# Layer two of a streaming-encoder trunk: two products of the values' pair between the gate block's halves, and the two 264-column blocks as one pair of seven products

## The chip, the cores and the metric

One core of one Trainium2 chip runs the whole program. The metric is device time in microseconds (us). TensorE (PE) multiplies; a matmul has a stationary operand loaded into the array ("LDWEIGHTS", PEld in the profile) and a moving one. VectorE (DVE) and ScalarE (ACT) do elementwise work, GpSimd (POOL) a few small operations and the stores of token sums, SyncE (SP) issues the loads.

## The reference

Two layers (DEPTH = 2) on x of 512 tokens by 2048 features. In each layer one input projection makes all of z = h @ w_in; the columns are queries, keys, values and gates of two head groups.

```python
def hybrid_layer(x, w_in, w_out, g_pre, g_post, w_alpha, b_alpha, g_gla, g_att, rel_bias):
    h = rmsnorm(x, g_pre)
    z = h @ w_in
    gq, gk, gv, gg, ga, aq, ak, av, ag = split_columns(z)
    log_a = jax.nn.log_sigmoid((ga @ w_alpha + b_alpha)) / GLA_TAU
    o_gla = gla_chunk_causal(gq, gk, gv, log_a)        # recurrence over chunks of 64 tokens
    o_gla = rmsnorm(o_gla, g_gla) * jax.nn.silu(gg)
    o_att = chunk_band_attention(aq, ak, av, rel_bias)  # softmax over 9 chunks
    o_att = rmsnorm(o_att, g_att) * jax.nn.silu(ag)
    y = jnp.concatenate([o_gla, o_att], axis=-1) @ w_out
    return x + rmsnorm(y, g_post)
```

## The kernel before

**Numbers.** Every product is made from high and low parts: a weight chunk w is cast to `wh` by ScalarE, VectorE makes `wl` = w − `wh`, and token operands are split in the same way (`split`, a ScalarE cast and a VectorE subtraction on line 109). A product then takes three matmuls: wh·a_hi, wl·a_hi, wh·a_lo. A weight chunk is 256 features (two runs of 128) by 512 columns, kept as a tile of 128 x 1024.

**Column blocks.** The input projection's columns are cut into blocks: AG0 (512 columns of the attention group's gates), AG1 and AG2 (264 columns each: the rest of the gates, and the 16 columns of the low-rank forget gate in AG2), and six pairs of 512-column blocks, `PAIRS`, the first of which, (AV0, AV1), is the attention values, the second and third the queries and keys.

**Two kinds of product.** `std_gemm` multiplies one block plainly: 8 chunks of features in the order `CO`, with 6 matmuls for each chunk and tile of 128 tokens (line 328). `fast_gemm` multiplies a pair of blocks by a scheme of seven products in place of eight: the tokens are cut into half 0 and half 1 (256 each), the features into a top and a bottom half, and the pair gives two column halves. P1 and P2 take the operands of half 0 and half 1 as they are, or weights added up; P5, P6, P3, P7 take sums and differences of token operands called S1, S2, S4, S3; P4 takes A22 itself. Each product runs over 4 chunks c0 to c3, so a pair is 28 jobs of 12 matmuls (line 406, or 396 when the roles of tokens and weights are exchanged). Accumulators X and Y (two PSUM tiles each) take turns, and finished products are copied out by ScalarE or combined by VectorE.

**Token operands.** Half 0's and half 1's operands are tiles named a11c, a12c (half 0) and g or sa tiles (half 1), made by `prep_half` from PE transposes. `make_sums` makes S1 to S4 for each chunk: a VectorE subtraction or addition (lines 588, 591, 594, 597), a split, and a store to DRAM on POOL's queue (S<-g). Some sums also keep a `home` in SBUF; the others go through slots named in `STAGE`, and each product that needs a sum reads it back on SP (sa<-S, ring of 4).

**Order of the work.** All weight chunks are jobs in one list, `stream`. `take` hands out the next job, and `ahead` keeps the coming jobs' loads (SP, into the ring raw of 5 or the ring H of 4), high parts (ring wh of 4) and low parts (ring wl of 3) three to five jobs ahead. Other work (sums, gates, attention) are generators in `tasks`, moved on by `pump` at a `rate` per step of a product. A scheduler below this language then fixes each engine's order. `tc.issue_after` forces one instruction behind another.

Layer two (l = 1) before: AG0 and AG1 over the two token tiles of half 0, the same over half 1 with the token sums as a task, AG2 over all four tiles with the last two chunks tile by tile (`lag=2`), then the task `forget_gate`, the load of ScalarE's table for exponentials (`act_table`), the values' pair, the query and key pairs, and the rest. In layer one the three blocks run over all four tiles, with the token sums beside AG1.

Of the kernel before, what the change touches and what calls it, by code (L numbers as in the profile page):

```python
# [16 lines left out]
L = 2  # L17
# [19 lines left out]
def hybrid_trunk(  # L37
# [109 lines left out]
    class Job:  # L147
        def __init__(self, l, kind, c, b0, b1=None, pair=None):
            self.l, self.kind, self.c, self.b0, self.b1, self.pair = l, kind, c, b0, b1, pair
            self.a = None  # L150

        def cut(self, tile_):
# [17 lines left out]
        def load(self):  # L170
            k, c, p, b0, b1 = self.kind, self.c, self.pair, self.b0, self.b1
            end = b0 >= NB_IN and k != "std"
            if end:
                c = OC[c]
            top, bottom = (c + 4, c) if end else (c, c + 4)
            mid = end and b0 == W23[0] and self.l < L - 1
            if k == "std":
                self.raw = self.fetch(rtile("raw", bufs=5), b0, c)
            elif k == "P1":
                p["H", self.c] = self.fetch(rtile("H"), b0, top)  # L180
                last_h[0] = last_load[0]
            elif k == "P5":
                p["r", self.c] = self.fetch(rtile("raw", bufs=5), b1, top)
            elif k == "P6":
                p["r", self.c] = self.fetch(rtile("raw", bufs=5), b1, bottom)
            elif k == "P7":
                p["r", self.c] = p.pop(("t", self.c), None) or self.fetch(rtile("raw", bufs=5), b0, top)
            elif k == "P2" or (k == "P4" and end):
# [3 lines left out]
            if src is not None and b0 != NB_IN and not (k == "P5" and b0 == AV0):  # L192
                until(lambda: k == "P4" or (id(sums), LEFT[k], c) in written)
                self.a = rtile("sa", (2, 512), F32R)
                with tc.issue_after(last_h[0]) if mid else nullcontext():
                    last_load[0] = nc.sync.dma_start(flat(self.a), src).ins
            if b0 == W23[0] and k == ("P6" if mid else "P5"):
                with tc.issue_after(last_h[0]):
                    p["t", self.c] = self.fetch(slot(f"a11{self.c}" if mid else SPARE[self.c], [2, 512]), b0, c + 4)

        def high(self):
            k, c, p = self.kind, self.c, self.pair
            if k == "std":
                src = self.raw
            else:
                h, r = p["H", c], p.get(("r", c))
                src = h if k in ("P1", "P5", "P6", "P4") else r
                early = k in ("P7", "P4") and self.b0 == W23[0] and self.l < L - 1
                with tc.issue_after(lows[-4 if early else -2]) if self.b0 >= NB_IN else nullcontext():
                    if k in ("P5", "P6") or (k == "P4" and self.b0 >= NB_IN):  # L210
                        nc.vector.tensor_tensor(out=h, in0=h, in1=r, op=ALU.add)  # L211
                    elif k == "P7":
                        nc.vector.tensor_tensor(out=r, in0=h, in1=r, op=ALU.subtract)  # L213
# [8 lines left out]
        def low(self):  # L222
# [7 lines left out]
            lows.append(last_low[0])  # L230
            if self.kind == "P2" and self.b0 < NB_IN:
                h = self.pair["H", self.c]
                nc.vector.tensor_tensor(out=h, in0=h, in1=self.src, op=ALU.add)  # L233

    stream = []
    for l in range(L):
        if l:
            stream += [Job(l, "std", c, b) for b in (AG0, AG1, AG0, AG1, AG2) for c in CO]
        else:
            stream += [Job(l, "std", c, b) for b in (AG0, AG1, AG2) for c in CO]  # L240
        for b0, b1 in PAIRS:
            pr = {}
            stream += [Job(l, k, c, b0, b1, pr) for k, c in PROD]
# [97 lines left out]

    def fast_gemm(l, pair, consume, rate=0.0, skip=0, feature_major=False, after=None, end=False, lag=0, ops=A):
        b0 = pair[0]
        acc = {n: [ps_mm.tile([P, W], F32, tag="mm", name=nm("mm")) for _ in range(2)] for n in roles[0]}
        roles.reverse()
        target = {"P1": "X", "P5": "Y", "P6": "X", "P3": "Y", "P7": "X", "P2": "Y", "P4": "X"}
        starts = ["P1", "P5", "P2"]
        if end:
            target.update(P2="Z")
        prod = (PROD_OUT if b0 == NB_IN else PROD_END) if end else PROD  # L350
        pace = Pace(rate, skip)
        keep = {}

        def copies(name, src):
            keep[name] = []
            for t in range(2):
                e = ev()
                last_copy[0] = nc.scalar.copy(e, src[t]).ins  # L358
# [8 lines left out]
        def finished(k, t):  # L367
            x_, y_ = acc["X"][t], acc["Y"][t]
            if k == "P3":
                consume(1, 0, t, None, combine(y_, keep["x"][t], ALU.subtract, keep["x"][t]))  # L370
            elif k == "P7":
                src = keep["x"][t] if end else x_
                consume(1, 1, t, None, combine(keep["p5"][t], src, ALU.subtract, keep["p5"][t]))
# [38 lines left out]
        for k, c in prod:  # L412
            if k == "P2" and end and c == 0:
                acc["Z"] = [aux(), aux()]
            if lag and k == "P4" and c == 4 - lag:
# [12 lines left out]
            if c == 3:  # L428
                if k == "P1":
                    copies("p1", acc["X"])  # L430
                elif k == "P5":
                    copies("p5", acc["Y"])
                elif k == "P6":
                    copies("x", acc["X"])
                else:
                    if k == "P7" and end:
                        copies("x", acc["X"])
                    for t in range(2):
# [31 lines left out]
    STAGE = ("g6", "g7", "g4", "g5", "g10")  # L470
    HOME = {("S1", c): tag for c, tag in enumerate(("g9", "g14", "g15", "g2"))}
    XS0 = (("g16", "g17"), ("g12", "g13"))
    XS1 = ("g9", "g10")
# [91 lines left out]

    def make_sums(dst, tags, parts, home={}, chunks=range(4)):
        stage = [0]

        def put(name, c, src):
# [10 lines left out]

        for c in chunks:
            got = parts(c)
            while got is None:
                yield
                got = parts(c)
            a11, a12, a21, a22 = got
            yield
            nc.vector.tensor_tensor(out=a22, in0=a21, in1=a22, op=ALU.subtract)
            put("S1", c, a22)
            yield  # L590
            nc.vector.tensor_tensor(out=a21, in0=a11, in1=a21, op=ALU.subtract)
            put("S3", c, a21)
# [8 lines left out]
    def token_sums(l):  # L601
        return make_sums(sa_d[l], STAGE, lambda c: (full[0, c][:, 0, :], full[0, c][:, 1, :], full[1, c][:, 0, :], full[1, c][:, 1, :]), HOME)

# [44 lines left out]
    def first_scales():  # L648
# [13 lines left out]
        nc.scalar.copy(rb, ps)  # L662

    def first_operands():
        ends = []
        for ch in CO:
# [71 lines left out]
    def layer(l):  # L738
# [111 lines left out]

        if l:
            for half in range(2):
                for q, b in enumerate((AG0, AG1)):
                    std_gemm(
                        l, b, (2 * half, 2 * half + 1), CO, operand_in, gate_evac(q), rate=0.7 if q else 1.3,
                    )
                if half == 0:
                    tasks.append(token_sums(l))
            std_gemm(l, AG2, range(NT), CO, operand_in, gate_evac(2), rate=0.7, lag=2)
        else:  # L860
# [4 lines left out]
        drain()  # L865
        tasks.append(forget_gate())
        act_table("natural_log_exp_and_others")

# [3 lines left out]
        def av_consume(j, h, t, src, comb):  # L872
            if (j, h) not in av:
                av[j, h] = slot(AVT[j][h], [2, 512])
            dst = av[j, h][:, t, :]
# [4 lines left out]

        fast_gemm(l, PAIRS[0], av_consume, rate=0.5)

# [537 lines left out]
        def finish(pair, xs):  # L1420
# [5 lines left out]
            yield from prep_half(l + 1, pair, xs)  # L1426
            if pair:
                yield from load_forget_gate(l + 1)

# [112 lines left out]
```

## Time and profile before

| | |
|---|---|
| runs | 1613.11, 1613.11, 1615.81 us, median 1613.11 |
| the profiled execution | 1617.0 us, its span 1615.2 us |
| granted TensorE clock, mean | 0.998 |
| DMA packets | 136075, 436.18 MB, mean 270 GB/s |
| ScalarE casts of weights (two groups) | 268.4 and 244.3 us busy |
| VectorE low parts of weights (two groups) | 312.0 and 281.5 us busy |

The shares of the page are means over stages with different limits, so the stage of layer two between 827 and 983 us, which the change rebuilds, is to be read by itself: by windows of busy time for each engine, and by PE's rows there with the idle time ahead of each and what ended it. The profiled execution is 3.9 us longer than the median.

### The profile page before, as it was taken

The page shows a single profiled execution, that of the slowest core. Times are in us where ns is not written, and L with a number is a line of the kernel's source. Part 1 is how long each engine was busy: PE and PEld are TensorE (multiplying, and loading weights), DVE is VectorE, ACT ScalarE, POOL GpSimd, SP SyncE. Part 2 cuts the span into 40 slices and gives each one's busy share as a digit, 9 for nine tenths or more (in the row PEclk, how much of TensorE's full clock was granted, in tenths as well). Part 3 has the DMA queues.
Part 4 walks back from the last instruction along what each step waited for, and adds up shares of the span by engine and source line. Part 5 has one row for each costly group of instructions (what it writes and reads, how often), then busy time and mean ns, then how long its engine had stood idle before and what let it go on. Part 6 is the DMA issues. An engine that isn't in the chain of part 4 may idle for free.

```text
span 1615.2 us, 25175 instructions
## 1 busy us (share of the span) xinstructions
PE 1600.0 (99%) x9206; PEld 1382.4 (86%) x9206; DVE 1268.8 (79%) x1675; ACT 914.4 (57%) x1521; POOL 131.3 (8%) x202
## 2 busy tenths in 40 slices
PE   9999999999999999999999999999999999999998
PEld 7988999998888778888888989999988877788886
DVE  5978768678677868988987677786786878689887
ACT  7554445657555546565785444456574545565655
POOL 0220000000010010100122000000000000101001
PEclk9999999999999999999999999999999999999999
DMA  9798686785868768689779686867858677686887
GB/s 350 238 406 305 216 290 212 232 305 170 280 215 289 257 218 312 236 305 376 272 249 398 242 300 222 296 205 240 310 211 275 223 282 260 218 307 237 329 304 211
DMA packets 136075, 436.18 MB, mean 270 GB/s; under 512 B 14756, under 2 KB 27300, under 8 KB 135920
## 3 DMA queue, kind: packets, MB, share of 16 engines
q1 hardware_dynamic: 119376, 374.74, 66.4%
q0 software_dynamic: 16288, 59.53, 10.1%
q8 instruction: 73, 1.20, 0.3%
q14 instruction: 50, 0.41, 0.1%
q10 hardware_dynamic: 288, 0.30, 0.1%
HBM read 374.99 MB, written 61.62 MB: 270 GB/s over the span
## 4 chain that ended last, share of the span: by engine, by line
PE 89%; DMA 4%; DVE 4%; issue 1%; ACT 1%; SPq 0%; POOLq 0%; DVEq 0%; ACTq 0%
PE mm L406 53%; PE mm L396 17%; PE mm L328 8%; PE ax L961 2%; PE ax L406 2%; DMA raw<-in_w_dram 2%; DVE wl L227 2%; DMA raw<-in_w_ag_dram 1%; PE ax L1147 1%; PE ax L944 1%; PE ax L1119 1%; PE ax L924 1%; PE ax L923 1%; PE ax L922 1%; ACT wh L217 0%
## 5 line engine op out<-in xcount | busy, mean ns | idle before, releaser
L406 PE MATMUL mm<-wh,sa 128*128 128x512 f32 x1600 | 517.3, 394 | 1.3 <-DMA sa<-S 0.7
L217 ACT CAST wh<-H 128x1024 fp32r<-128x1024 f32 x256 | 268.4, 1051 | 216.0 <-PE mm L406 93.7
L227 DVE TENSOR_TENSOR wl<-H,wh 128x1024 fp32r<-128x1024 f32 x256 | 312.0, 1221 | 90.1 <-PE mm L406 28.3
L217 ACT CAST wh<-raw 128x1024 fp32r<-128x1024 f32 (+2 forms) x249 | 244.3, 986 | 215.7 <-PE mm L406 85.0
L406 PEld LDWEIGHTS mm<-wh,sa 128*128 128x128 f32 x1600 | 299.5, 188 | 73.4 <-issue 9.2
L227 DVE TENSOR_TENSOR wl<-raw,wh 128x1024 fp32r<-128x1024 f32 (+2 forms) x249 | 281.5, 1134 | 76.0 <-PE mm L406 26.0
L406 PE MATMUL mm<-wl,sa 128*128 128x512 f32 x800 | 312.9, 391 | 0.0
L396 PE MATMUL mm<-sa,wh 128*128 128x256 f32 x1280 | 237.9, 285 | 0.4 <-DMA sa<-S 0.4
L406 PE MATMUL mm<-wh,a 128*128 128x512 f32 x640 | 211.9, 394 | 0.0
L396 PEld LDWEIGHTS mm<-sa,wh 128*128 128x128 f32 x1280 | 200.4, 191 | 1.0 <-issue 0.5
L396 PE MATMUL mm<-sa,wl 128*128 128x256 f32 x640 | 181.5, 284 | 0.8 <-DVE wl L227 0.7
L211 DVE TENSOR_TENSOR H<-H,raw 128x1024 f32<-128x1024 f32 x144 | 174.9, 1219 | 1.9 <-DMA raw<-in_w_dram 1.0
L406 PEld LDWEIGHTS mm<-wl,sa 128*128 128x128 f32 x800 | 150.3, 188 | 30.4 <-DVE wl L227 0.7
L406 PEld LDWEIGHTS mm<-wh,a 128*128 128x128 f32 x640 | 119.4, 188 | 25.0
L406 PE MATMUL mm<-wl,a 128*128 128x512 f32 x320 | 125.7, 393 | 0.0
L396 PEld LDWEIGHTS mm<-sa,wl 128*128 128x128 f32 x640 | 122.4, 191 | 1.4 <-DVE wl L227 1.4
L448 POOL TENSOR_TENSOR sm<-sm,mhalf 128x2 f32<-128x2 f32 (+2 forms) x40 | 50.5, 1261 | 743.1 <-DVE sm L971 437.8
L213 DVE TENSOR_TENSOR raw<-H,raw 128x1024 f32<-128x1024 f32 x56 | 68.4, 1224 | 50.8 <-DMA raw<-in_w_dram 50.8
L406 PE MATMUL mm<-wh,g 128*128 128x512 f32 x320 | 101.9, 392 | 0.0
L396 PE MATMUL mm<-a,wh 128*128 128x256 f32 x512 | 94.9, 285 | 0.0
L358 ACT COPY ev<-mm 128x512 f32<-128x512 f32 x104 | 60.9, 585 | 58.3 <-PE mm L406 42.7
L233 DVE TENSOR_TENSOR H<-H,raw 128x1024 f32<-128x1024 f32 x48 | 58.7, 1223 | 42.4 <-DMA raw<-in_w_dram 42.4
(255 smaller groups left out, 2400.8 us busy)
## 6 DMA issues: line engine op xcount, KB each, us to landing
raw<-in_w_dram SPq DMA_DIRECT2D x287, 512.0 KB, 5.3
sa<-S SPq DMA_DIRECT2D x184, 512.0 KB, 4.5
H<-in_w_dram SPq DMA_DIRECT2D x64, 512.0 KB, 4.8
sa<-A SPq DMA_DIRECT2D x48, 512.0 KB, 5.9
S<-g POOLq DMA_DIRECT2D x32, 512.0 KB, 9.5
sa<-oS SPq DMA_DIRECT2D x32, 512.0 KB, 5.4
raw<-in_w_ag_dram SPq DMA_DIRECT2D x40, 264.0 KB, 4.9
oS<-g POOLq DMA_DIRECT2D x16, 512.0 KB, 4.7
```

What stands on the lines that cost most here:

```text
L211: nc.vector.tensor_tensor(out=h, in0=h, in1=r, op=ALU.add)
L213: nc.vector.tensor_tensor(out=r, in0=h, in1=r, op=ALU.subtract)
L217: last_cast[0] = nc.scalar.copy(self.wh[:, z, :], src[:, z, :]).ins
L227: last_low[0] = nc.vector.tensor_tensor(out=self.wl[:, z, :], in0=self.src[:, z, :], in1=self.wh[:, z, :].bitcast(F32), op=ALU.subtract).ins
L233: nc.vector.tensor_tensor(out=h, in0=h, in1=self.src, op=ALU.add)
L328: nc.tensor.matmul(pss[o], a(part, kk, o) if callable(a) else a[:, part, t], rhs[:, kk, :], start=(i == 0 and kk == 0 and m == 0), stop=(i ...
L358: last_copy[0] = nc.scalar.copy(e, src[t]).ins
L396: nc.tensor.matmul(dst, lhs[:, kk, f], a[:, part, tok], start=(fresh and kk == 0 and m == 0 and ft % 2 == 0), stop=(c == 3 and kk == 1 and ...
L406: last_mm[0] = nc.tensor.matmul(out_ps[t], a[:, part, tok], rhs[:, kk, :], start=(fresh and kk == 0 and m == 0), stop=(c == 3 and kk == 1 ...
L448: nc.gpsimd.tensor_tensor(out=out_r, in0=v, in1=mhalf[:, : v.shape[-1]], op=ALU.pow)
L922: nc.tensor.matmul(ps[:, :n], self.qh[:, t], self.kh[:, :n], start=True, stop=False)
L961: nc.tensor.matmul(o, self.pt[i][:, j * P : (j + 1) * P], av[hd // 4, j // 2][:, j % 2, (hd % 4) * P : (hd % 4 + 1) * P], start=(j == 0), ...
```

## The change

Layer two only, but for the last point:

- AG0 over half 0 is followed by eight products of the values' pair, P2 and P1 over c0 to c3 (`PROD_FRONT`); they use half 0's operands alone. Then AG0 over half 1 runs, and then the pair's other 20 jobs (`PROD_REST`: P5, P6, P3, P7, P4). The pair's weights for P1 stay in four slots, P2's finished product is copied out, and P5 and P3 accumulate in two auxiliary PSUM banks (Z). The sums S1 and S2 stay in SBUF as well (`HOMES`), and the sums' other stores go through three staging slots.
- AG1 and AG2 run last, as a pair of seven products (`GATE_PAIR`, `PROD_GATE`), 28 jobs of 12 matmuls of 264 columns in place of 2 blocks of 8 chunks by 4 token tiles by 6 matmuls: 336 for 384. Then `load_forget_gate`, `forget_gate` and the table load follow, and the query and key pairs.
- In layer one the sums' additions and subtractions are put behind the last operand split (`behind`).

```diff
+    PROD_FRONT = order("20 21 22 23 10 11 12 13")
+    PROD_REST = order("50 51 52 53 60 61 30 62 63 31 70 32 71 72 73 33 40 41 42 43")
+    PROD_GATE = order("10 11 50 12 51 13 52 60 53 61 30 62 31 63 32 70 33 71 20 72 21 73 22 23 40 41 42 43")
+    GATE_PAIR = (AG1, AG2)
...
+            self.parted = l == L - 1 and kind != "std" and b0 == AV0
...
             elif k == "P1":
-                p["H", self.c] = self.fetch(rtile("H"), b0, top)
+                h = slot(f"g{4 + c}", [2, 512]) if self.parted else rtile("H")
+                p["H", self.c] = self.fetch(h, b0, top)
...
+            if self.l == L - 1:
+                home = k in ("P5", "P6") and b0 in (AV0, AG1)
+            else:
+                home = k == "P5" and b0 == AV0
+            if src is not None and b0 != NB_IN and not home:
...
         if l:
-            stream += [Job(l, "std", c, b) for b in (AG0, AG1, AG0, AG1, AG2) for c in CO]
+            pr = {}
+            stream += [Job(l, "std", c, AG0) for c in CO]
+            stream += [Job(l, k, c, *PAIRS[0], pr) for k, c in PROD_FRONT]
+            stream += [Job(l, "std", c, AG0) for c in CO]
+            stream += [Job(l, k, c, *PAIRS[0], pr) for k, c in PROD_REST]
+            pr = {}
+            stream += [Job(l, k, c, *GATE_PAIR, pr) for k, c in PROD_GATE]
...
-    def make_sums(dst, tags, parts, home={}, chunks=range(4)):
+    def make_sums(dst, tags, parts, home={}, behind=None):
         stage = [0]
+
+        def sub(out, a, b):
+            with tc.issue_after(behind()) if behind else nullcontext():
+                nc.vector.tensor_tensor(out=out, in0=a, in1=b, op=ALU.subtract)
...
+        tags, home = (("g10", "g16", "H"), HOMES) if l else (STAGE, HOME)
+        return make_sums(sa_d[l], tags, lambda c: (...), home, None if l else lambda: ends[-1])
...
-        if l:
-            for half in range(2):
-                for q, b in enumerate((AG0, AG1)):
-                    std_gemm(
-                        l, b, (2 * half, 2 * half + 1), CO, operand_in, gate_evac(q), rate=0.7 if q else 1.3,
-                    )
-                if half == 0:
-                    tasks.append(token_sums(l))
-            std_gemm(l, AG2, range(NT), CO, operand_in, gate_evac(2), rate=0.7, lag=2)
...
+        if l:
+            std_gemm(l, AG0, (0, 1), CO, operand_in, gate_evac(0), rate=1.3)
+            roles.reverse()
+            acc = {n: [ps_mm.tile([P, W], F32, tag="mm", name=nm("mm")) for _ in range(2)] for n in "YX"}
+            fast_gemm(l, PAIRS[0], av_consume, rate=2.5, prod=PROD_FRONT, acc=acc)
+            until(lambda: all((kh, 1, c) in A for kh in range(2) for c in range(4)))
+            tasks.append(token_sums(l))
+            std_gemm(l, AG0, (2, 3), CO, operand_in, gate_evac(0), rate=0.9)
+            fast_gemm(l, PAIRS[0], av_consume, rate=1, prod=PROD_REST, acc=acc)
+            drain()
+            fast_gemm(l, GATE_PAIR, gate_consume, prod=PROD_GATE)
+            tasks.append(load_forget_gate(l))
+            tasks.append(forget_gate())
+            act_table("natural_log_exp_and_others")
+        else:
+            fast_gemm(l, PAIRS[0], av_consume, rate=0.5)
```

By each engine's order the program has 48 matmuls fewer; ScalarE has 14 instructions more (4 casts of 528 columns, 8 copies of finished 264-column products, 2 of 512), VectorE 26 (16 sums of 528 columns, 4 low parts, 6 combinations of 264), SP 8 loads (4 fewer of gate weights, 4 more each of pair weights, of A22, and of sums).

At the end of AG0 over half 0, PE went on with AG1's 264 columns (a110 and a123 are operands of half 0, the tile after MATMUL is the accumulator):

```order
L328 MATMUL mm_1603_8243<-wl_1628_8372,a123_1592_8196 128x512
L328 MATMUL mm_1603_8243<-wh_1626_8349,a123_1592_8196 128x512
L328 MATMUL mm_1664_8530<-wh_1629_8374,a110_1563_8075 128x264
L328 MATMUL mm_1665_8531<-wh_1629_8374,a110_1563_8075 128x264
L328 MATMUL mm_1664_8530<-wl_1639_8423,a110_1563_8075 128x264
```

In the changed kernel P2 of the values' pair stands there, on operand a120:

```order
L344 MATMUL mm_1603_8243<-wl_1628_8372,a123_1592_8196 128x512
L344 MATMUL mm_1603_8243<-wh_1626_8349,a123_1592_8196 128x512
L431 MATMUL mm_1662_8526<-wl_1639_8423,a120_1571_8097 128x512
L431 MATMUL mm_1662_8526<-wh_1629_8374,a120_1571_8097 128x512
L431 MATMUL mm_1663_8527<-wl_1639_8423,a120_1571_8097 128x512
L431 MATMUL mm_1663_8527<-wh_1629_8374,a120_1571_8097 128x512
```

So 512-column matmuls with half 0's operands stand between the two halves of AG0, where 264-column ones stood.

ScalarE at the end of the gate blocks, before (from AG2 to the values' pair; t2 is the silu's output, mm the accumulator, wh a weight's high part):

```order
L217 CAST wh_1781_9218<-H_1779_9190 128x1024
L217 CAST wh_1784_9248<-H_1782_9220 128x1024
L745 ACTIVATE t2_1786_9264<-mm_1764_9068 128x248
L745 ACTIVATE t2_1788_9284<-mm_1765_9069 128x248
L745 ACTIVATE t2_1789_9302<-mm_1766_9070 128x248
```

The same engine after (from the gate pair to the first query and key pair, whose first weight is H_1910):

```order
L775 ACTIVATE t2_1912_9841<-ev_1839_9448 128x264
L804 CAST g13_1939_9972<-g12_1938_9971 98x512
L775 ACTIVATE t2_1927_9921<-mm_1818_9331 128x264
L227 CAST wh_1914_9858<-H_1910_9834 128x1024
L775 ACTIVATE t2_1928_9924<-mm_1819_9332 128x264
L62 ACT_TABLE_LOAD
```

Two casts of the next pair stood ahead of the last silus; now the first cast stands behind the silu of the first accumulator of P4 (mm_1818), and ahead of the second.

VectorE in layer one, before (L109 is a split's subtraction, a113 an operand of half 0, wl_144 a low part of AG1; L588 a subtraction of a sum; L677 scales the tokens):

```order
L109 TENSOR_TENSOR g9_140_821<-g14_67_383,g9_140_821 128x512
L109 TENSOR_TENSOR g6_141_832<-g14_67_383,g6_141_832 128x512
L227 TENSOR_TENSOR wl_144_864<-raw_133_776,wh_138_816 128x528
L109 TENSOR_TENSOR a113_127_740<-H_126_737,a113_127_740 128x512
L677 SCALAR_TENSOR_TENSOR H_126_737<-g13_76_432,gcol_172,bias_3_178 128x256 x2
L588 TENSOR_TENSOR g2_119_696<-g2_119_696 128x512
L109 TENSOR_TENSOR g5_148_888<-g15_110_643,g5_148_888 128x512
```

And after:

```order
L109 TENSOR_TENSOR a123_130_763<-H_126_737,a123_130_763 128x512
L237 TENSOR_TENSOR wl_150_909<-raw_139_818,wh_145_866 128x528
L109 TENSOR_TENSOR sa_134_780<-g3_128_749,sa_134_780 128x512
L599 TENSOR_TENSOR g14_67_383<-g14_67_383 128x512
L599 TENSOR_TENSOR g15_110_643<-g15_110_643 128x512
```

Splits of operands (a113 here) stood among the sums (L588 and the splits of g9, g6, g5); now the first sums (L599) stand behind all of them.

More of the change, by code (lines that the diff above doesn't have):

```diff
@@ L230, in low @@
             lows.append(last_low[0])
-            if self.kind == "P2" and self.b0 < NB_IN:
+            if self.kind == "P2" and self.b0 < NB_IN and not self.parted:
                 h = self.pair["H", self.c]
@@ L340, in hybrid_trunk, with fast_gemm @@
     roles = ["XY", "YX"]
-    def fast_gemm(l, pair, consume, rate=0.0, skip=0, feature_major=False, after=None, end=False, lag=0, ops=A):
+    def fast_gemm(l, pair, consume, rate=0.0, skip=0, feature_major=False, after=None, end=False, lag=0, ops=A, prod=None, acc=None):
         b0 = pair[0]
-        acc = {n: [ps_mm.tile([P, W], F32, tag="mm", name=nm("mm")) for _ in range(2)] for n in roles[0]}
-        roles.reverse()
+        gates = b0 == AG1
+        wide = N1 if gates else W
+        parted = acc is not None
+        if not parted:
+            acc = {n: [ps_mm.tile([P, W], F32, tag="mm", name=nm("mm"))[:, :wide] for _ in range(2)] for n in roles[0]}
+            roles.reverse()
         target = {"P1": "X", "P5": "Y", "P6": "X", "P3": "Y", "P7": "X", "P2": "Y", "P4": "X"}
         starts = ["P1", "P5", "P2"]
-        if end:
+        if end or gates:
             target.update(P2="Z")
-        prod = (PROD_OUT if b0 == NB_IN else PROD_END) if end else PROD
+        if parted:
+            target.update(P5="Z", P3="Z")
+        if prod is None:
+            prod = (PROD_OUT if b0 == NB_IN else PROD_END) if end else PROD
         pace = Pace(rate, skip)
@@ L412, in fast_gemm @@
         for k, c in prod:
-            if k == "P2" and end and c == 0:
-                acc["Z"] = [aux(), aux()]
+            if k == "P2" and (end or gates) and c == 0 or k == "P5" and parted and c == 0:
+                acc["Z"] = [aux()[:, :wide], aux()[:, :wide]]
             if lag and k == "P4" and c == 4 - lag:
@@ L873, in av_consume @@
             if (j, h) not in av:
-                av[j, h] = slot(AVT[j][h], [2, 512])
+                av[j, h] = slot("g17" if l and not (j or h) else AVT[j][h], [2, 512])
             dst = av[j, h][:, t, :]
```

62 lines of the change are left out of this document (31 added, 31 removed).

## The prediction

> **What bounds the kernel now.** I read the page's first lines, the stretch of layer two that the change rebuilds, then PE's rows wherever PE idles there.
>
> ```profile
> span 1615.2 us, 25175 instructions
> PE 1600.0 (99%) x9206; PEld 1382.4 (86%) x9206; DVE 1268.8 (79%) x1675; ACT 914.4 (57%) x1521; POOL 131.3 (8%) x202
> PE 89%; DMA 4%; DVE 4%; issue 1%; ACT 1%; SPq 0%; POOLq 0%; DVEq 0%; ACTq 0%
> ```
>
> PE works in 1600 of 1615.2 us and makes 89% of the chain: fewer matmuls shorten the run, and only about 15 us of idling can be won besides. The same by stretch:
>
> ```profile
> core 0: us, PE busy (x) PEld busy (x) DVE busy (x) ACT busy (x) POOL busy (x), PEclk, DMA share, GB/s
> 827.00:845.00 18.00, 17.12 (x137) 16.48 (x136) 14.37 (x24) 16.61 (x36) 2.74 (x5) 1.00 0.83 282
> 845.00:866.00 21.00, 21.00 (x95) 17.38 (x95) 20.12 (x28) 13.32 (x21) 7.05 (x14) 1.00 1.01 381
> 866.00:884.00 18.00, 15.48 (x119) 14.42 (x117) 10.28 (x16) 8.13 (x16) 5.31 (x10) 1.00 1.03 413
> 884.00:907.00 23.00, 22.45 (x171) 22.36 (x172) 9.29 (x19) 8.51 (x14) 1.64 (x3) 0.93 1.01 377
> 907.00:930.00 23.00, 23.00 (x105) 18.96 (x104) 21.53 (x23) 13.26 (x17) 1.11 (x2) 1.00 0.39 127
> 935.00:960.00 25.00, 25.00 (x112) 20.72 (x111) 16.82 (x16) 10.93 (x12) 0.00 (x0) 1.00 0.87 303
> ```
>
> From 827 to 907 layer two runs AG0 and AG1 over half 0, AG0 and AG1 over half 1, then AG2; from 907 the values' pair. PE idles 0.88 us in the first row, 2.52 in the third, 0.55 in the fourth, and there its clock averaged 0.93. From 845 to 907 the DMA engines are full.
>
> ```profile
> 842.75 0.62 PE L328 MATMUL mm<-wh,g 128*128 128x512 f32 x2
> 844.25 0.50 PE L328 MATMUL mm<-wl,g 128*128 128x512 f32 x1 [0.88 <-DVE wl L227]
> 875.03 0.51 PE L328 MATMUL mm<-wh,g 128*128 128x264 f32 x2 [0.43 <-ACT wh L217]
> 880.80 0.28 PE L328 MATMUL mm<-wh,g 128*128 128x264 f32 x1
> 880.92 0.28 PE L328 MATMUL mm<-wl,g 128*128 128x264 f32 x1
> 884.55 0.69 PE L328 MATMUL mm<-wh,a 128*128 128x264 f32 x2 [2.14 <-ACT wh L217]
> 885.49 0.42 PE L328 MATMUL mm<-wl,a 128*128 128x264 f32 x1
> 885.71 0.64 PE L328 MATMUL mm<-wh,a 128*128 128x264 f32 x2
> DMA packets 5093, 15.43 MB, mean 396 GB/s; under 512 B 600, under 2 KB 600, under 8 KB 5090
> S<-g POOLq DMA_DIRECT2D x16, 512.0 KB, 9.3
> raw<-in_w_ag_dram SPq DMA_DIRECT2D x14, 264.0 KB, 9.5
> 883.87 0.63 ACT L217 CAST wh<-raw 128x528 fp32r<-128x528 f32 x1 [4.26 <-DMA raw<-in_w_ag_dram]
> ```
>
> These are PE's rows, the DMA answer for 845 to 884 us, and ScalarE's row ahead of PE's longest wait. A 264-column matmul starts 0.12 us after the one before (880.80, 880.92), so a 12-matmul job lasts 1.44 us. At 884.55 PE had waited 2.14 us for a cast that had waited 4.26 us for weights: the 16 stores of token sums (S<-g) fill the DMA engines, and narrow weights land after 9.5 us. After that wait a matmul takes 0.22 us (885.49 to 885.71).
>
> **The change, part by part.** The sum is made on the profiled execution, 1617.0 us around its span; the median of the runs, 1613.1, lies 3.9 below it, and I apply the differences to the median.
>
> *Products.* AG1 and AG2 were 2 × 16 jobs' worth of token halves, 384 matmuls; 28 jobs of 12 are 336. 48 × 0.12 = −5.8 us. Eight half-one products of the values' pair only move. Added: 16 VectorE sums of 528 columns, 4 more lows and 6 combinations of 264, 14 more ScalarE instructions; they are inside the budgets below.
>
> *Stall at 843.* There AG0 over half 1 needs its weights' low part while VectorE also makes sums and half-1 operands; AG1 gave it 96 × 0.12 = 11.5 us of cover. A 512-column matmul takes 25.00/112 = 0.22 us by the row 935 to 960, a job of 12 about 2.7. Now the eight front products stand there, 21.6 us: −0.9 (the idle 0.88; between −0.9 and 0).
>
> *AG1 and AG2 under the stores.* The idle 2.52 + 0.55 goes, since 2.7-us jobs now stand under the stores: −3.1. The low clock costs 0.07 × 23 = 1.6 us by the fourth row, and its cause goes with the wait: −1.6.
> [...]
>
> *Layer one.* The sums' VectorE subtractions now stand behind the last operand split.
>
> ```profile
> 70.00:76.00 6.00, 5.15 (x37) 4.48 (x36) 5.97 (x12) 4.36 (x9) 1.51 (x3) 1.00 0.84 305
> 73.54 0.51 PE L328 MATMUL mm<-wh,a 128*128 128x264 f32 x2 [0.42 <-DVE a L109]
> ```
>
> PE idles 0.85 us here with VectorE full at 5.97 of 6, half of it for an operand split that the sums delay: −0.8. Ends: −1.4 (with gaps nearby) and +1.0, if sums pushed back delay weights like the 0.88 at 844.25.
>
> *The 20 remaining products with the sums (REST).* The operations' distances on VectorE:
>
> ```profile
> 836.93 0.68 DVE L109 TENSOR_TENSOR sa<-g,sa 128x512 fp32r<-128x512 f32 x1
> 837.53 0.68 DVE L591 TENSOR_TENSOR g<-H,g 128x512 f32<-128x512 f32 x1
> 842.98 1.22 DVE L227 TENSOR_TENSOR wl<-raw,wh 128x1024 fp32r<-128x1024 f32 x1
> 844.12 0.69 DVE L109 TENSOR_TENSOR sa<-g,sa 128x512 fp32r<-128x512 f32 x1
> ```
>
> 0.60 us for a narrow one, 1.14 for a wide one. By the order, from the front's second product to the low part of the last P6 VectorE has 32 wide and 41 narrow operations, 61 us. PE reaches that product after 59.4 us (22 jobs less 0.4), and the ring of three lets a low run ahead by two jobs less its own 1.14, 4.3 us: a margin of 2.7. The row 907 to 930 shows VectorE at 21.53 of 23 without an idle PE, the row 866 to 884 a PE idle for 14%; 14% of 59.4 is 8.3. Between 0 and +8.3 I take +1.0, nearer the first, because the jobs are wide.
>
> *The gate pair.* Its 28 jobs take 40.7 us on PE, and VectorE needs 32 of these, ScalarE 25. Transfers: 20 weight loads (0.27 MB) and 12 sums read back (0.52 MB), 11.7 MB, with 2.6 to 4.7 MB for the QK pair behind: 350 to 403 GB/s. Landing times of the whole run:
>
> ```profile
> sa<-S SPq DMA_DIRECT2D x184, 512.0 KB, 4.5
> raw<-in_w_ag_dram SPq DMA_DIRECT2D x40, 264.0 KB, 4.9
> 878.60 0.39 ACT L745 ACTIVATE t<-mm 128x264 f32<-128x264 f32 x1
> L217 ACT CAST wh<-H 128x1024 fp32r<-128x1024 f32 x256 | 268.4, 1051 | 216.0 <-PE mm L406 93.7 <-PE mm L396 50.8 <-DVE H L211 46.4
> ```
>
> A read of a sum into the ring of four is covered by three jobs, 4.35 us: about enough for 4.5, not for 9.5. Lower end 0; upper end three rounds of the ring at 9.5 − 4.35, 15.5 us. The nearest row, AG2's stretch, lost 3.1 + 1.6 under the stores, which are over by now: +2.0, some 40% of it.
> [...]
>
> *Seam into the QK pair.* ScalarE's first cast for it is ordered behind the silu of P4's first token tile, which needs P4's end. PE then waits for a silu (0.39 at 878.60), a cast (1.05) and part of the low (1.22): about 2.1 us; 0 if the trace's order gives way, 3.0 with the second silu ahead. Before, two casts stood ahead of the gate block's silus. +2.1.
>
> *At nothing.* The forget gate's tasks move from the values' pair to the QK pair, under PE-bound work (row 935 to 960: VectorE 16.82 of 25, ScalarE 10.93). Four more reads of each kind on SP in REST are in its wide jobs.
>
> Sum: −5.8 − 0.9 − 3.1 − 1.6 − 0.8 + 1.0 + 2.0 + 2.1 = −7.1, so 1606.0 us.
>
> **The rivals.**
> *The gate pair starves.* 1.44-us jobs with a transfer of 0.27 to 0.52 MB each are the shape that starved under the stores; the DMA share already is 1.01 in such a stretch. Against it: no stores run now, and reads land in 4.5 us. At 9.5 us the loss is 15.5 in place of 2.0: 1619.5, slower. It decides from a landing of about 8.5 us, where three rounds cost 12.5 and eat the gain of 9.1 and 3.2 more.
> *REST is bound by VectorE.* For it: the margin of 2.7 us, and 3 staging slots where there were 5, each held for a 9.3-us store. Against it: eight staged sums through three slots need 8/3 × 9.3 = 25 us of 59. Price 8.3 in place of 1.0: 1613.3, no change.
> *Only the products count.* Each wait that goes comes back in the gate pair and the seam: 1613.1 − 5.8 = 1607.3. For it: 5.1 us of new waits stand against 6.4 removed. That the matmuls themselves stay is excluded by the order: PE has 48 fewer.
>
> **How the numbers follow.** 0.2%, or 3.2 us, is about what a measurement of this kernel can tell from no change. Forecast 0.57 (within it, small errors of each term), products alone 0.20, REST bound 0.12, gate pair starved 0.11. Faster: the first two, 0.77; same: REST bound, 0.12; slower: 0.11. The low end, 1600, is the sum without the three new costs (1600.9) and with layer one's −1.4; the high end, 1613, reaches to REST's case. It leaves out the starved pair and the edges.
>
> **What would show it.** PE has 48 matmuls fewer, and 264-column jobs of layer two start 1.44 us apart. No wait above 0.5 us at the change from front to AG0's second half, and no PEclk below 1 in AG0 or REST: else terms two to four are wrong. In REST, PE idles about 1 us; long waits for wl or H would make it VectorE's. In the gate pair, waits named sa or raw with landings above 5 us are the starved case. At the seam PE waits about 2 us for wh. In layer one the 0.42 wait for an operand is gone. The prediction fails outright if the gate pair's clock falls: at 0.22 us per matmul over a third of its 40.7 us, the loss would be 6 us, more than the products save.

## The result and the profile after

| | time, median | against before |
|---|---|---|
| before | 1613.11 us (1613.10 to 1615.81) | |
| changed | 1626.21 us (1625.29 to 1627.0) | ratio 1.0077, 95% interval 1.0059 to 1.0094 |

The changed kernel is 13.1 us slower; 1606.0 was predicted, 1600 to 1613 the range. Its page begins:

```profile
span 1624.6 us, 25125 instructions
PE 1600.1 (98%) x9158; PEld 1378.9 (85%) x9158; DVE 1284.1 (79%) x1701; ACT 921.8 (57%) x1535; POOL 129.8 (8%) x202
PE 85%; DMA 5%; issue 4%; DVE 4%; ACT 1%; POOL 0%; POOLq 0%; SPq 0%; DVEq 0%; ACTq 0%
```

The 48 matmuls are gone (9206 to 9158 records), yet PE is busy as long as before, and its part of the chain falls from 89% to 85%: waits, and matmuls at a lower clock, have taken the place of the work removed. There are three places. First layer one, by windows (columns as in the prediction), where before PE was full; the rows of before, then of the changed kernel:

```profile
100.00:110.00 10.00, 10.00 (x47) 8.09 (x46) 6.81 (x10) 3.83 (x5) 1.08 (x2) 1.00 1.03 417
110.00:121.00 11.00, 11.00 (x49) 8.84 (x49) 8.18 (x9) 5.61 (x7) 0.59 (x1) 1.00 1.02 415
```

```profile
100.00:110.00 10.00, 8.24 (x34) 5.41 (x33) 9.56 (x12) 5.60 (x8) 2.51 (x5) 1.00 1.02 416
110.00:121.00 11.00, 6.17 (x24) 4.52 (x23) 4.71 (x5) 1.99 (x2) 0.76 (x2) 0.84 1.03 420
121.00:135.00 14.00, 14.00 (x57) 11.36 (x56) 11.15 (x11) 8.16 (x10) 0.00 (x0) 0.88 0.41 132
```

PE idles 1.76 + 4.83 us, and the clock of 0.84 and 0.88 costs up to 1.8 + 1.7 more. (Here and below, the price of the clock is one minus PEclk, times the window. It counts low-clock time in which PE waits as well, so it is an upper bound: here the clock was at half from 117.5 to 124.4 us, the first 1.7 us of them still within the wait, and the price is 2.5 in place of 3.5.) The DMA engines were full there before too; what is new is how late a load enters them. The changed kernel's timeline follows that wait back:

```profile
99.50 0.68 DVE L625 TENSOR_TENSOR H<-H,g 128x512 f32<-128x512 f32 x1
106.02 0.62 ACT L108 CAST g<-H 128x512 fp32r<-128x512 f32 x1 [2.93 <-DMA S<-g]
107.74 0.68 DVE L109 TENSOR_TENSOR g<-H,g 128x512 fp32r<-128x512 f32 x1
108.45 0.33 SPq L172 DMA_DIRECT2D H<-in_w_dram  x1
118.18 1.99 ACT L227 CAST wh<-H 128x1024 fp32r<-128x1024 f32 x2 [9.64 <-DMA H<-in_w_dram]
119.27 1.22 PE L431 MATMUL mm<-wh,a 128*128 128x512 f32 x2 [4.83 <-ACT wh L227]
```

The last S4 is made at 99.50. Its split needs a staging slot and waits until 106.02 for the store (S<-g) that holds it; the split's second half reads H at 107.74. Only then is that tile of ring H free, and the values' pair's load is issued at 108.45, lands 9.6 us later among full DMA engines, is cast at 118.18, and PE goes on at 119.27. Before, the same rows are 10 to 13 us earlier:

```profile
89.82 0.69 DVE L597 TENSOR_TENSOR H<-H,g 128x512 f32<-128x512 f32 x1
95.27 1.27 SPq L167 DMA_DIRECT2D H<-in_w_dram  x1
```

The transfer itself is not slower than before: the two H loads issued in that stretch landed after 15.6 us in the median before, after 9.6 in the changed kernel. It is the issue that is late.

Second and third, layer two, by windows of the changed kernel:

```profile
850.00:875.00 25.00, 25.00 (x112) 20.68 (x111) 22.13 (x29) 15.34 (x21) 3.19 (x6) 1.00 0.70 233
875.00:900.00 25.00, 21.86 (x89) 17.39 (x88) 23.99 (x28) 12.01 (x17) 4.81 (x9) 0.93 1.01 381
900.00:925.00 25.00, 24.48 (x106) 19.15 (x105) 19.24 (x20) 12.82 (x17) 2.92 (x6) 1.00 1.01 379
925.00:950.00 25.00, 25.00 (x139) 21.67 (x138) 19.14 (x25) 10.74 (x16) 0.00 (x0) 1.00 0.83 299
965.00:985.00 20.00, 17.91 (x147) 17.51 (x145) 14.83 (x36) 9.42 (x19) 3.52 (x7) 1.00 1.01 392
985.00:1005.00 20.00, 17.46 (x120) 16.89 (x121) 14.11 (x14) 11.15 (x13) 1.41 (x3) 0.83 0.93 356
```

Beside the 20 products PE idles 3.14 + 0.52 us with VectorE at 23.99 of 25, and loses 0.07 × 25 = 1.75 to the clock. At the end of the gate pair and the seam it idles 2.09 + 2.54 and loses up to 0.17 × 20 = 3.4 (3.0 without the time in which PE waits). PE's waits, SP's queue and ScalarE at the seam:

```profile
891.83 0.50 PE L431 MATMUL mm<-wl,g 128*128 128x512 f32 x1 [3.14 <-DVE wl L237]
970.22 0.49 PE L431 MATMUL mm<-wh,sa 128*128 128x264 f32 x2 [0.84 <-DMA sa<-S]
986.75 0.36 PE L431 MATMUL mm<-wh,sa 128*128 128x264 f32 x1 [3.00 <-DMA sa<-A]
989.50 1.22 PE L421 MATMUL mm<-a,wh 128*128 128x256 f32 x4 [0.75 <-ACT wh L227]
...
971.42 2.41 SPq L172 DMA_DIRECT2D raw<-in_w_dram  x3
973.93 0.60 SPq L206 DMA_DIRECT2D sa<-A  x1
974.63 1.46 SPq L172 DMA_DIRECT2D raw<-in_w_dram  x2
976.52 0.33 SPq L206 DMA_DIRECT2D sa<-A  x1
...
988.12 0.39 ACT L775 ACTIVATE t<-mm 128x264 f32<-128x264 f32 x1 [4.39 <-PE mm L431]
988.41 1.04 ACT L227 CAST wh<-H 128x1024 fp32r<-128x1024 f32 x1
```

Three 512-KB loads for the next pair went in ahead of the last but one read of A22, and two more ahead of the last; that one, issued at 976.52, let PE go on at 986.75, 10.2 us later. After the waits of 3.14 and 3.00 the clock fell.

### The profile page after: what moved, and what is told of

Read it like the earlier page. It is cut to its first block, busy times and chain, and to the rows that moved or that the text cites. A ratio compares the mean times of both kernels' runs of the same rounds, so it can differ in the third digit from the quotient of the medians.

```text
span 1624.6 us, 25125 instructions
## 1 busy us (share of the span) xinstructions
PE 1600.1 (98%) x9158; PEld 1378.9 (85%) x9158; DVE 1284.1 (79%) x1701; ACT 921.8 (57%) x1535; POOL 129.8 (8%) x202
## 4 chain that ended last, share of the span: by engine, by line
PE 85%; DMA 5%; issue 4%; DVE 4%; ACT 1%; POOL 0%; POOLq 0%; SPq 0%; DVEq 0%; ACTq 0%
PE mm L431 50%; PE mm L421 18%; PE mm L344 5%; PE ax L431 3%; DMA raw<-in_w_dram 3%; PE ax L1000 2%; DVE wl L237 2%; PE ax L1186 1%; PE ax L983 1%; PE ax L1158 1%; DMA sa<-S 1%; PE ax L963 1%; PE ax L962 1%; PE ax L961 1%; DMA sa<-A 1%
## 5 line engine op out<-in xcount | busy, mean ns | idle before, releaser
L431 PE MATMUL mm<-wh,sa 128*128 128x512 f32 (+1 forms) x1632 | 517.6, 388 | 5.2 <-DMA sa<-A 3.0
L227 ACT CAST wh<-H 128x1024 fp32r<-128x1024 f32 (+1 forms) x256 | 261.5, 1024 | 212.5 <-PE mm L431 88.7
L237 DVE TENSOR_TENSOR wl<-H,wh 128x1024 fp32r<-128x1024 f32 (+1 forms) x256 | 303.5, 1188 | 97.6 <-PE mm L431 35.8
L431 PE MATMUL mm<-wl,sa 128*128 128x512 f32 (+1 forms) x816 | 313.9, 385 | 0.3 <-DVE wl L237 0.3
L431 PE MATMUL mm<-wh,a 128*128 128x512 f32 (+1 forms) x672 | 219.8, 392 | 5.9 <-ACT wh L227 5.9
L221 DVE TENSOR_TENSOR H<-H,raw 128x1024 f32<-128x1024 f32 (+1 forms) x144 | 170.3, 1188 | 1.0
L431 PE MATMUL mm<-wl,a 128*128 128x512 f32 (+1 forms) x336 | 131.1, 391 | 0.3 <-DVE wl L237 0.3
L431 PE MATMUL mm<-wh,g 128*128 128x512 f32 (+1 forms) x384 | 115.8, 378 | 0.4 <-ACT wh L227 0.4
L223 DVE TENSOR_TENSOR raw<-H,raw 128x1024 f32<-128x1024 f32 (+1 forms) x56 | 66.4, 1186 | 45.0 <-DMA raw<-in_w_dram 42.8
L381 ACT COPY ev<-mm 128x512 f32<-128x512 f32 (+1 forms) x112 | 64.0, 571 | 54.9 <-PE mm L431 39.5
L243 DVE TENSOR_TENSOR H<-H,raw 128x1024 f32<-128x1024 f32 (+1 forms) x48 | 56.7, 1181 | 42.0 <-DMA raw<-in_w_dram 41.5
```

The lines of the kernel that those rows point to most:

```text
L227: last_cast[0] = nc.scalar.copy(self.wh[:, z, :], src[:, z, :]).ins
L237: last_low[0] = nc.vector.tensor_tensor(out=self.wl[:, z, :], in0=self.src[:, z, :], in1=self.wh[:, z, :].bitcast(F32), op=ALU.subtract).ins
L431: last_mm[0] = nc.tensor.matmul(out_ps[t], a[:, part, tok], rhs[:, kk, :], start=(fresh and kk == 0 and m == 0), stop=(c == 3 and kk == 1 ...
```

## The experiments

Each was run against the kernel before on its chip; the median of before was 1613.31, 1612.69 and 1612.78 us in the three groups. Times are medians over all executions of a run; rows and windows come from one profiled execution of it.

**Layer one: undone, and alone.** First, in the changed kernel:

```diff
-        return make_sums(sa_d[l], tags, ..., home, None if l else lambda: ends[-1])
+        return make_sums(sa_d[l], tags, ..., home)
```

> The changed kernel with layer one's sums no longer held behind the last operand split; layer two as changed. Theory A (holding the sums back shifts layer one's stores into the start of the values' pair, so its H loads land late): the trace of the changed kernel is 6.9 us later than before at the same point ahead of layer two, so about 1626.2 - 6.9 = 1619 us (1617 to 1621), and no PE wait above 1 us between 95 and 125 us. Theory B (the lost time is all layer two's, the wait in layer one is made up elsewhere): 1624 to 1627.

1615.31 us, ratio 1.0016 (1.0007 to 1.0026): 10.9 below the changed kernel, and below theory A's 1617 to 1621. From 100 to 121 us PE is full again. (This kernel is called the first run below.) Second, the same hold in the kernel before and nothing else:

```diff
-            nc.vector.tensor_tensor(out=a22, in0=a21, in1=a22, op=ALU.subtract)
+            sub(a22, a21, a22)    # issue_after(ends[-1]) in layer one; a21 likewise
```

> The kernel before, with only layer one's sums held behind the last operand split; layer two as before. Theory A: 1613.1 + 6.9 = 1620 us (1618 to 1623), with a PE wait of some 5 us for an H load near 115 us. Theory B: within 2 us of 1613.

1621.43 us, ratio 1.0052 (1.0037 to 1.0067): 8.1 us slower, with a clock of 0.84 and 0.88 in the same two windows, and the wait:

```profile
120.76 0.73 PE L406 MATMUL mm<-wh,a 128*128 128x512 f32 x2 [3.18 <-ACT wh L217]
```

So theory A holds: most of the 13.1 us comes from the hold on layer one's subtractions. Only the two that make S1 and S3 are held, for each of the four chunks; S2 and S4 are made from their results and so come later too. B is out. That the staging slots and their stores are the link in between is read from the trace; no run gave these sums more slots.

**Layer two: the front alone, the gate pair alone.**

```diff
+            stream += [Job(l, "std", c, b) for b in (AG1, AG1, AG2, AG2) for c in CO]
             stream += [Job(l, k, c, *PAIRS[0], pr) for k, c in PROD_REST]
...
-            stream += [Job(l, k, c, *GATE_PAIR, pr) for k, c in PROD_GATE]
```

> Layer one as before; layer two with the eight front products between AG0's halves, but AG1 and AG2 plain (each half of the tokens by itself, 32 narrow jobs) ahead of the pair's other 20 products, and S2 read back from memory. Against the first of these runs it has 48 matmuls of 0.12 us more (+5.8) and no gate pair (its waits and the low clock there cost 1.0 + 3.2 + 1.5 + 3.4 = 9 us). Theory C (the gate pair is what loses in layer two): 1619 - 9 + 5.8 = 1616 (1613 to 1618). Theory D (the front and the sums beside the 20 products lose): no better than the first run, 1619 or more.

1624.21 us, ratio 1.0076 (1.0059 to 1.0093): 8.9 above the first run. The time lies where D has it, but most of the waits stand beside the plain narrow blocks: in the window below, PE idles 4.72 of 16 us with the DMA engines full at 1.04, and the longest wait is 2.65 us for a wh, at 898.07. From 965 to 985 us, where by the counts of matmuls the 20 products run, it idles 3.17 us. The run also differs by more than the missing pair: its sums go through two staging slots in place of three.

```profile
884.00:900.00 16.00, 11.28 (x79) 10.06 (x78) 7.83 (x13) 7.15 (x14) 3.20 (x6) 0.97 1.04 396
```

Then the gate pair without the front:

```diff
             stream += [Job(l, "std", c, AG0) for c in CO]
-            stream += [Job(l, k, c, *PAIRS[0], pr) for k, c in PROD_FRONT]
             stream += [Job(l, "std", c, AG0) for c in CO]
-            stream += [Job(l, k, c, *PAIRS[0], pr) for k, c in PROD_REST]
+            stream += [Job(l, k, c, *PAIRS[0], pr) for k, c in PROD]
```

In this one the undivided pair's P1 weights are in ring H again, the sums go through six staging slots, and AG0's second half has a task rate of 2.0.

> Layer one as before; layer two with AG0 over both halves, then the values' pair undivided with the token sums, then the gate pair of seven products. No front products. Theory C: the gate pair's 9 us of waits stay, 1619 or more. Theory D: the waits near 890 to 920 us (3.3 + 0.4 + 0.5) go and those of the gate pair are small, so 1613 to 1616.

1635.82 us, ratio 1.0143 (1.0128 to 1.0159). D is out. The gate pair's wait for A22 stands here too (3.33 us, at 998 us), as C has it, but most of the loss is neither C's nor D's: PE waits for weights in H:

```profile
861.54 1.22 PE L430 MATMUL mm<-wh,a 128*128 128x512 f32 x2 [7.83 <-ACT wh L227]
889.19 1.22 PE L430 MATMUL mm<-wh,a 128*128 128x512 f32 x2 [7.79 <-ACT wh L227]
```

This is layer one's mechanism: the token tiles of half 0 hold ring H until their S4 is split. The front puts the pair's P1 weights into the slots g4 to g7, and that, besides the cover, is what it seems to bring. Taken apart, each half of the change, as built here, is worse than both together.

**A second execution of before.**

> The kernel before once more, unchanged, for a second profiled execution. If the waits between 874 and 888 us and the low clock there (3.1 + 1.6 us) belong to every execution, they stand in this one too, at the same size; if they belong to the slow execution of 1617.0 us that was read, this one lies near 1613 and shows half of them or less.

1614.65 us, a single execution. The stretch that the prediction read shows less:

```profile
866.00:884.00 18.00, 16.42 (x127) 15.53 (x125) 11.43 (x18) 9.08 (x17) 5.96 (x12) 1.00 1.03 412
884.00:907.00 23.00, 23.00 (x177) 22.21 (x177) 10.68 (x21) 10.02 (x15) 2.16 (x4) 1.00 1.04 405
883.33 0.50 PE L328 MATMUL mm<-wh,a 128*128 128x264 f32 x2 [1.39 <-ACT wh L217]
```

Idle 1.58 in place of 3.07, the longest wait 1.39 in place of 2.14, and the clock did not fall.

**The end of the gate pair: order of reads.** All that follows has layer one's sums free.

```diff
+            if self.l == L - 1 and self.b0 == PAIRS[1][0]:
+                with tc.issue_after(gate_read[0]):    # the gate pair's last read of A22
+                    self.load_()
```

> The first run's kernel (layer one's sums free) with the loads of the first query and key pair of layer two put behind the gate pair's last read of A22. Theory E (five 512-KB weight loads, issued for the next pair ahead of the last two reads of A22, make PE wait 3.4 us and halve its clock at the end of the gate pair): that wait falls below 0.5 us, about 1615.3 - 3.4 - 1.7 = 1610 (1609 to 1612). Theory F (the wait only moves, since the next pair's own loads then land late): a wait for H or raw of 2 us or more after the seam, 1614 to 1616.

1620.56 us, ratio 1.0045 (1.0031 to 1.0058): 5 us worse than without. A22's wait went, and the next pair's weights were late:

```profile
977.96 0.74 PE L431 MATMUL mm<-a,wh 128*128 128x256 f32 x4 [1.06 <-ACT wh L237]
982.89 0.74 PE L431 MATMUL mm<-a,wh 128*128 128x256 f32 x4 [1.02 <-ACT wh L237]
988.60 0.74 PE L431 MATMUL mm<-a,wh 128*128 128x256 f32 x4 [1.79 <-ACT wh L237]
```

The waits move, as theory F has it, though none reaches its 2 us, and the time lies above its 1614 to 1616. Where the 5 us are lost is not shown: in the profiled execution, 1617.53 us, idle and clock from 815 to 995 us are 8.9 + 1.7, less than the first run's 7.6 + 5.1, and PE idles 3.4 us more than there in stretches that the edit does not touch.

**Less VectorE work, and sums sooner.**

```diff
-            sub(a21, a11, a21)
+            if dst is not sa_d[L - 1]:
+                sub(a21, a11, a21)    # the addition of S4 likewise
```

> The first run's kernel without the subtraction of S3 and the addition of S4 in layer two (8 narrow VectorE operations, 4.8 us of VectorE; the splits, stores and reads of both stay, so S3 and S4 hold other values). Theory G (VectorE is the bound beside the 20 products): the wait of 3.5 us for a low part at 879 us falls below 0.5, and with it the clock of 0.85 and 0.81 around it (3.4 us): 1615.3 - 6.5 = 1609 (1608 to 1611). Theory H (the stores of sums or late weights are the bound): the wait stays, 1614 to 1616.

1616.32 us, ratio 1.0021 (1.0011 to 1.0031): the total did not fall. Beside the 20 products PE's idle and the clock did improve, 875 to 895 us (the first run's rows, then this one's):

```profile
875.00:885.00 10.00, 6.71 (x26) 5.06 (x25) 10.00 (x12) 4.46 (x6) 2.90 (x6) 0.85 1.03 406
885.00:895.00 10.00, 10.00 (x38) 8.06 (x37) 9.70 (x13) 5.96 (x9) 2.12 (x4) 0.81 1.00 322
975.00:985.00 10.00, 7.26 (x44) 6.96 (x45) 4.09 (x5) 5.69 (x7) 1.67 (x3) 0.83 1.03 412
```

```profile
875.00:885.00 10.00, 8.83 (x39) 6.67 (x37) 10.00 (x12) 5.47 (x7) 3.55 (x7) 1.00 1.03 419
885.00:895.00 10.00, 9.02 (x39) 7.02 (x40) 9.19 (x11) 4.75 (x7) 1.60 (x3) 1.00 1.05 402
975.00:985.00 10.00, 6.99 (x29) 6.42 (x30) 3.87 (x4) 5.40 (x7) 1.15 (x3) 0.56 1.03 415
```

3.29 idle and 3.4 of clock became 2.15 idle, 4.5 us won. From 965 to 995 us, at the pair's end, idle and clock together grew from 5.0 (0.55 + 2.74 + 1.7) to 9.6 (4.53 + 5.1): the gain was lost again 90 us later. So G is right on its place, though the longest wait left there is 0.98 where it has 0.5, and wrong on the total.

Then sums sooner, in the kernel with the reads first:

```diff
-            std_gemm(l, AG0, (2, 3), CO, operand_in, gate_evac(0), rate=0.9)
+            std_gemm(l, AG0, (2, 3), CO, operand_in, gate_evac(0), rate=1.6)
```

> The kernel of the second of these runs (reads first) with the rate of tasks in AG0's second half at 1.6 in place of 0.9, so that the token sums are written earlier and stand ahead of more of the weights' operations on VectorE. Theory G: sums pulled into a stretch where VectorE has 12 to 17% idle shorten the wait at 879 us, 1 to 5 us below the second run. Theory H: the wait stays or grows, since the stores come closer together; no better than the second run.

1616.69 us, ratio 1.0018 (1.0008 to 1.0028), 3.9 below the kernel it is built on, within what G expected. From 875 to 895 us PE idles 2.28 with a full clock, where that kernel has 3.17 and 1.7.

**Holds and rings.** Layer two's splits no longer behind the last cast:

```diff
-            with tc.issue_after(last_cast[0]):
+            with tc.issue_after(last_cast[0]) if dst is not sa_d[L - 1] else nullcontext():
                 split(op[:, 0, :], op[:, 1, :], src)
```

> The first run's kernel (layer one's sums free), with the splits of layer two's sums no longer held behind the last weight cast; by the order the first of them then stands 17 places earlier on VectorE. Theory G2 (beside the 20 products VectorE is late since the sums start late: the first subtraction is at 835.8 us, its split at 855.4): the wait of 3.5 us near 880 us halves and the low clock there goes, 1615.3 - 4 = 1611 (1610 to 1613). Theory H (the stretch is full of transfers, whatever VectorE does): 1614 to 1617.

1614.32 us, ratio 1.0012 (0.9999 to 1.0024). PE's idle from 875 to 895 us is 0.99 with a full clock, for 3.29 and 3.4, as G2 has it; but the gate pair's end loses more, 5.1 idle and 5.1 of clock from 955 to 985 us for the first run's 4.2 and 1.7, and the time misses G2's 1610 to 1613. Why the end gets worse is not shown. Next, that end alone:

```diff
-                h = slot(f"g{4 + c}", [2, 512]) if self.parted else rtile("H")
+                h = slot(f"g{4 + c}", [2, 512]) if self.parted or b0 == AG1 else rtile("H")
```

> The first run's kernel, with the gate pair's four P1 weights in the slots g4 to g7 in place of the ring H, so that the first query and key pair finds the ring free. Theory K (the end of the gate pair is a hand-over of rings within four jobs of 1.44 us: first the reads of A22, then the H loads are late, whichever goes second): the H loads go early, the wait at the seam goes, that for A22 (3.4 us) stays, 1613 to 1616. Theory L (only the number of bytes matters): no change in the sum of the waits between 955 and 995 us (5.9 us with the clock).

1612.24 us, ratio 0.9995 (0.9985 to 1.0004). From 975 to 995 us PE is full at clock 1.00: both waits went, more than K expected. PE's order changed with the edit: the next pair's first products now stand ahead of P4's last job (its first row is the second here):

```profile
979.50 0.65 PE L421 MATMUL mm<-a,wh 128*128 128x256 f32 x4
985.74 0.29 PE L431 MATMUL mm<-wh,sa 128*128 128x264 f32 x1
```

So the last read of A22, which is issued at 972.81 behind five loads for the next pair as in the first run, has 12.9 us to land, where PE in the first run was waiting 7.2 us after the issue. Waits for sa<-S, 1.28 and 0.84 us, came up beside the products instead. With the P5 loads behind A22 too:

```diff
             elif k == "P5":
-                p["r", self.c] = self.fetch(rtile("raw", bufs=5), b1, top)
+                with tc.issue_after(gate_read[0]) if self.l == L - 1 and b0 == PAIRS[1][0] else nullcontext():
+                    p["r", self.c] = self.fetch(rtile("raw", bufs=5), b1, top)
```

> The run before in this list, with the first P5 weights of the next pair behind the last read of A22 as well. Theory K: now both have room, the waits of A22 and of the seam fall below 1 us together and the clock stays full, 1615.3 - 5 = 1610 (1609 to 1612). Theory L: the waits move to raw after the seam, 1614 or more.

1613.40 us, ratio 1.0004 (0.9993 to 1.0015): no better than the run before, so this edit alone adds nothing once ring H is free; K's 1609 to 1612 is missed, though the pair's end idles only 1.1 us from 955 to 995. And all three:

> The run before in this list, with the splits of layer two's sums unheld as in the first. Theories G2 and K together: 1615.3 - 9 = 1606 to 1608, faster than before by 5 to 7. If H or L hold: 1612 to 1616.

**1605.20 us, ratio 0.9955 (0.9941 to 0.9968)**: 7.6 us faster than before, some 21 faster than the change as made, and a little below what G2 and K together gave. Its windows:

```profile
845.00:865.00 20.00, 20.00 (x90) 16.57 (x89) 19.90 (x26) 13.41 (x18) 4.40 (x9) 1.00 0.88 320
885.00:895.00 10.00, 9.20 (x40) 7.62 (x41) 10.00 (x11) 5.77 (x8) 1.06 (x2) 1.00 1.04 398
895.00:915.00 20.00, 20.00 (x90) 16.55 (x89) 14.59 (x13) 8.92 (x11) 0.26 (x1) 1.00 0.98 386
975.00:985.00 10.00, 9.33 (x78) 9.12 (x78) 8.57 (x10) 5.09 (x7) 0.00 (x0) 1.00 1.03 416
```

VectorE is at 19.90 of 20 from 845 to 865 us, where PE had cover, and nowhere from 815 to 995 does the clock fall. In the first run and in this one PE's idle and the clock's loss over that stretch are 7.6 + 5.1 and 2.5 + 0: 10.2 less, and the medians differ by 10.1. Alone, the splits gave 1.0 and the own slots 3.1, and the order of the P5 loads on top of the slots gave nothing; together they gave 10. With the splits alone, 5.7 us were won beside the products and 4.3 lost at the pair's end; with the slots alone, some 5 were won at the end and 0.8 lost beside the products. Splits and slots without the order of loads were not run, so whether the last run needs it stays open.

## Why the prediction was wrong, point by point

- *Products*, −5.8: the count is right (9158 records).
- *Stall at 843*, −0.9: right. From 850 to 875 us PE is at 25.00 of 25, and no wait shows at the change from the front to AG0's second half.
- *AG1 and AG2 under the stores*, −3.1 − 1.6: mechanism right, size wrong. It was read from one execution 3.9 us above the median; the second shows 1.58 idle and a full clock. About −1.6.
- *Layer one*, −0.8 within −1.4 and +1.0: **this is the step that failed**. It measures +8.1 alone. The gain it took is there (PE idles 0.85 us less from 70 to 85 us, and the 0.42 wait is gone), but some 9 us of waits and low clock follow 30 us later. The text took the operand split that would come sooner, and for the upper end a wait of 0.88 for a low part; it did not ask what is queued behind the sums that come later: their stores, the staging slots, and through S4's split the ring H, whose next loads feed the values' pair.
- *REST*, +1.0 within 0 and +8.3: the mechanism, VectorE without margin, was right; it measures 3.66 idle and 1.75 of clock in the changed kernel, 5.4. The margin of 2.7 counted VectorE as always having work; the hold behind the last cast left VectorE idle 12% from 850 to 875 and full after it, which the freed splits show.
- *Gate pair and seam*, +2.0 + 2.1: both waits came, and with the clock they measure 2.09 + 2.54 + 3.0 = 7.6. The landing was taken too short: the last A22 needed 10.2 us, beyond the 4.5 of the sum and the 9.5 of the rival. And the clock after a wait, seen once at 884 us, was not added to new waits, though the prediction named a falling clock in this pair as its last sign; it fell at the pair's end. The seam's cause was only partly the silu: in the first run the cast stands ahead of it, and A22's wait stays at 3.26.

−5.8 − 0.9 − 1.6 + 8.1 + 5.4 + 7.6 = +12.8, against 13.1 measured. That it comes so close is partly luck: the 8.1 is a difference of medians, the others are read from single executions. For the first run the same sum, with 7.6 idle and 4.6 of clock (5.1 less the time in waits), is −8.3 + 12.2 = +3.9, against 2.0: single executions differ by waits of about 1 us elsewhere, so it holds to some 2 us. The hold costs 8.1 in the kernel before and 10.9 in the changed one. In layer one the two agree: the 800th matmul, which stands behind the stall, starts at 145.94 us in the first run and at 154.01 in the changed kernel, 8.1 later, and at 146.29 and 155.17 before and with the hold alone, 8.9 later. The other 3 us are lost in layer two, where the text of the two kernels is the same; which wait they come from stays open, and part may be the seam, whose order differs between them.

The rival of a starved gate pair had the right sign and too small a place; no rival stood for layer one. The last run's 1605.2 lies near the 1606.0 of the forecast, but it does not confirm it: that kernel has three edits more and layer one's hold less. It shows that a gain of the size of the layer-two terms was within reach.

## What to carry to other kernels

Before holding an instruction back, list the buffers that its readers free, and follow the next load into each of them to the engine that needs it; the cost comes out there (here the first held subtraction is at 69 us and PE's wait ends at 119), not where the hold is. When a stage with long jobs is followed by one with short jobs, count the hand-over of each ring in jobs of the short kind. Read a wait from two executions before it is written into a sum.

## What was not expected of the hardware

- Some PE waits cost more than their own length. After waits of 2.14 us (before, at 884.55), 3.14 and 3.00 (the changed kernel, at 891.83 and 986.75), 3.29 (the first run, at 882.97) and 4.83 us (the changed kernel, at 119.27) the clock was at half for 3.4 or 6.8 us, which cost 1.7 to 3.0 us more; after single waits of 1.39 (the second execution of before, at 883.33) and 1.79 (the run with the reads first, at 988.60) it stayed full. The length of one wait did not decide it: in the run with the gate pair alone, matmuls that started 0.23 us apart (866.06, 866.29) started 0.43 us apart (870.07 to 871.35) after waits of 1.42 and 0.21 us; the longer wait before them, 7.83 us, had ended at 861.54. The clock records between 50 and 1010 us have one low stretch of 3.4 us in the kernel before, and stretches of 6.8, 3.4 and 6.8 us in the changed kernel; the windows of the run with less VectorE work, 0.56 and 0.93 from 975 to 995 us, make 10.2 us.
- The DMA engines of this one core moved 410 to 420 GB/s over tens of microseconds (85 to 121 us of the changed kernel: 410, 416 and 420 by its windows); what suffered was the landing of a 512-KB read, 4.5 us in the median of the sums read back over the whole run, and 9.6 and 10.2 for the reads issued at 108.45 and 976.52 us, with a DMA share of 1.03 (110 to 121 us) and 1.02 (976.5 to 987).
